# Moving the last group of adaLN weight loads and sums into the second block's input projection

## The chip, the cores and the metric

One Trainium2 chip, one core. The metric is the device time of one execution in microseconds: the median over the runs shown, beside one execution taken with the hardware profiler. Engines are named as in the profile: PE is TensorE, DVE is VectorE, ACT is ScalarE, POOL is GpSimd and SP is SyncE, which here issues all DMAs of the kernel. L1253 is line 1253 of the kernel before.

## The reference, cut to what matters

The kernel computes one hybrid decoder layer on x of 1024 tokens by 1024 channels in float32. The conditioning vector c gives six vectors of 1024 channels, and these shift, scale and gate the two halves of the layer:

```python
mod = silu(c) @ ada_w + ada_b
shift1, scale1, gate1, shift2, scale2, gate2 = split(mod, 6)
h = x * (1.0 + scale1) + shift1
z = h @ w_in                                 # 1024 x 3984
o = concat(hgrn2(z_h), gla(z_g), rwkv7(z_r)) @ w_out
x = layer_norm(ALPHA * x + (1.0 + gate1) * o)
h = x * (1.0 + scale2) + shift2
m = square(relu(h @ mlp_w_up)) @ mlp_w_down
x = layer_norm(ALPHA * x + (1.0 + gate2) * m)
```

The sixth vector, gate2, is needed only in the last line. The change moves the work that computes it.

## The kernel before, in words

The tokens go through in two blocks of 512, each of four tiles of 128. For each block there is an input projection (`z_block`, `z_rest`, `z_last`), the three mixers (`mix`, one tile after another with state carried along, in stages that overlap two tiles), the output projection with layer norm (`out_block`), and the MLP. Results of the input projection go to DRAM (`zr`, `zgc`, `zgt`, `zhc`, `zht`), and the mixers load them from there; they store theirs to `oD`, from which the output projection loads.

Every large product is made of three matmuls in a reduced float32 format. A weight slab of 128 rows is loaded (`slab`, tile `raw`, five buffers), ScalarE rounds it (`wh`, L1287), and VectorE takes the remainder (`wl`, L1288; four buffers of each). TensorE then does high by high, high by low and low by high (L1337 to L1339). The PSUM tile `dn` has four buffers. When a product is done, its tiles are copied, by ScalarE (L1382) and in the first block by VectorE in turn (L1384), to the tile `s2` (two buffers; the profile calls it `s`), and stored (L1386, L1388).

The six vectors of the conditioning are computed on VectorE. The weights come transposed, so that channel group q, 128 channels of the 6144, is one load of 128 by 1024 floats (512 KB) and one instruction that multiplies it by silu(c) and sums along the row:

```python
w = self.dt([P, D], "xt", 4)
ins = nc.sync.dma_start(w, self.A["ada_wt"][q * P:(q + 1) * P, :])
nc.vector.scalar_tensor_tensor(w, w, 1.0, self.cact, ALU.mult, ALU.mult, accum_out=self.sums[:, q:q + 1])
```

`xt` has four buffers, and silu(c) holds one of them until the last sum; three rotate among the loads. The first 16 channel groups (shift1 and scale1) are loaded in step with the first block's projection (`ada_first`). The other 32, eight for each of the four remaining vectors m = 2, 3, 4, 5, come from `ada_later(m)`, called in the program after the first block's mixers. For m = 2 and m = 5 (the gates) it also transposes the result in PSUM (tile `ml`, L1273) and stores it as a row to DRAM. Later `xt` tiles, in program order, are those of the output block (`ys`) and of the MLP.

The order in which instructions stand on each engine is not that of the program. At the end, `Order` lists all instructions with their dependences, walks through them with its own table of durations, and fixes one order for each engine, which the hardware then follows. An instruction's rank is its level (`level(n)`, lower first) and then its place in the program. ScalarE and VectorE take ready instructions that touch the dense products' pools (`feeds`, and `xt` is one of these pools' tiles) ahead of all others. Buffers of one tag are handed out in program order. Levels here: the first block's projection -1, its rest (`z_rest`) 0.5, the first block's mixers 0, the second block's projection 2 (`L_Z1`), `ada_later` 3 (`L_ADA`), the output block 0. So the second block's projection is the filler for the time of the first block's mixers, and the loads of `ada_later` go out whenever SP has nothing of a lower level to issue and an `xt` buffer is free.

ScalarE's two sets of activation tables are loaded in program order too (`act`): the exponentials of a stage stand behind the sigmoids of that stage, the last of which, of the tile G (L330), needs what the first block's projection stored last.

Of the kernel before, what the change touches and what calls it, by code (L numbers as in the profile page):

```python
# [25 lines left out]
KT = D // P  # L26
# [93 lines left out]
class Kern:  # L120
# [5 lines left out]
    def init(self, tc, ctx):  # L126
        self.tc, self.nc = tc, tc.nc
        self.psm = ctx.enter_context(tc.tile_pool(name="psm", bufs=2, space=PSUM))
        self.mp = ctx.enter_context(tc.tile_pool(name="mp", bufs=1))
        self.nid = 0  # L130
        self.table, self.head, self.group = None, None, []
        self.later, self.levels, self.first = [], [], None

# [1042 lines left out]
class Full(Kern):  # L1176
# [68 lines left out]
        self.sums = self.cp.tile([P, 48], F32, name="sums")  # L1245


    def ada_sum(self, q):
        nc = self.nc
        w = self.dt([P, D], "xt", 4)  # L1250
        ins = nc.sync.dma_start(w, self.A["ada_wt"][q * P:(q + 1) * P, :])
        self.first = ins if q == FIRST else self.first
        nc.vector.scalar_tensor_tensor(w, w, 1.0, self.cact, ALU.mult, ALU.mult, accum_out=self.sums[:, q:q + 1])  # L1253

# [8 lines left out]
            self.ada_sum(q)  # L1263
            self.ada_end(q, 1, plus)

    def ada_later(self, m):
        nc = self.nc
        for j in range(KT):
            self.ada_sum(8 * m + j)
        self.ada_end(8 * m, KT, 0.0 if m % 3 == 0 else 1.0)  # L1270
        if m % 3 == 2:
            ps = self.lps()
            nc.tensor.transpose(ps[0:8, 0:P], self.mod[:, 8 * m:8 * m + 8], self.ident)  # L1273
            row = self.dt([P, 512], "lnr", 2)[0:8, 0:P]
            nc.scalar.copy(row, ps[0:8, 0:P])
            nc.sync.dma_start(self.gD[m].rearrange("o (j p) -> (o j) p", p=P), row)
# [14 lines left out]
    def slab(self, ap, eng=None, tag="w"):  # L1291
        n = ap.shape[1]
        raw = self.dt([P, 512], "raw", RB)
        self.nc.sync.dma_start(raw[:, 0:n], ap)
        return self.split(raw[:, 0:n], tag, AB if tag == "a" else WB, n, eng=eng)


# [308 lines left out]
def build(tc, A):  # L1606
    with ExitStack() as ctx:
        k = Full(ctx, tc, A)
        k.level(-1)
        k.scratch()  # L1610
        k.ada_setup()
        k.z_block(0)
        k.level(0)
        k.setup_consts(A["consts"])
        k.level(L_Z0)
        k.z_rest(0)
        k.level(0)
        k.setup_mixers(A["masks"], A["wau"],
                       A["gla_alpha_up"][0], A["rwkv_g_up"][0], (A["rwkv_gn_g"], A["rwkv_gn_b"]))
        k.mix(0, M0)  # L1620
        k.level(L_ADA)
        for m in (2, 3, 4, 5):
            k.ada_later(m)
        k.level(L_Z1)
        k.z_block(1)
        k.z_rest(1)
        k.level(0)
        ys = k.out_block(0, False)
        k.z_last(1, (k.x_moving(1, j, True) for j in range(KT)))
        h = k.mlp_moving(ys, False)  # L1630
        k.mix(1, M1)
        k.tail(ctx)
        nch = FT // 4
        acc = [k.dt([P, D], "xt", 4) for _ in range(TPB)]
        for fc in range(nch):
            k.level(L_MLP + fc)
            k.mlp_chunk(fc, h, acc, False)
            if fc == OUT_AT:
                ys = k.out_block(1, True, L_MLP + fc + 2)
            k.level(L_MLP + fc + 1)  # L1640
            if fc == MOVE_AT:
                h1 = k.mlp_moving(ys, True)
        acc1 = [k.dt([P, D], "xt", 4, late=True) for _ in range(TPB)]
        k.level(L_MLP + nch)
        for fc in range(nch - 1):
            k.mlp_chunk(fc, h1, acc1, True)
            if fc == 0:
                k.level(L_MLP + nch + 1)
                k.mlp_end(0, acc)
                k.level(L_MLP + nch)  # L1650
        k.mlp_last(1, h1, acc1)
        Order(tc, k.later, k.levels).apply()
# [37 lines left out]
```

## Time and profile before

| | |
|---|---|
| median of 3 runs | 1487.52 us (1486.14 to 1488.55) |
| profiled execution | 1486.98 us |
| its span | 1485.2 us |
| mean granted TensorE clock | 0.981 |
| PE busy | 1406.1 us (95%) |
| DVE busy | 1055.1 us (71%) |
| ACT busy | 708.9 us (48%) |
| HBM read and written | 180.03 MB and 32.06 MB |

The times are of whole executions. The profiled one stands 1.8 us above its span, and 0.54 us below the median of the runs. The busy shares are averages over stages that differ: in the first 160 us the DMA engines are nearly full, from 220 to 480 us the mixers of the first block run beside the second block's projection, and beyond 600 us the MLP fills TensorE. What a moved piece of work costs or gives back has to be read from its own stage.

### The profile page before, as it was taken

What the parts mean: (1) busy time and instruction counts of PE and PEld (TensorE: products, weight loads), DVE (VectorE), ACT (ScalarE), POOL (GpSimd) and SP (SyncE); (2) the same over time, 40 slices, a digit from 0 to 9 for tenths busy, and PEclk for the clock granted to TensorE, in tenths of its full rate; (3) what the DMA queues carried; (4) which work ended last, traced back from release to release, by engine and by line L of the source; (5) the groups of instructions that cost most, each with busy time, mean ns of one, the idle gap of its engine ahead of it and who ended that gap; (6) DMA issues with size and microseconds to landing.
All of it is one profiled execution on the core that took longest, in us unless ns stands there. A gap on an engine that the chain in (4) does not pass through costs nothing.

```text
span 1485.2 us, 29273 instructions
## 1 busy us (share of the span) xinstructions
PE 1406.1 (95%) x11226; PEld 1124.2 (76%) x11226; DVE 1055.1 (71%) x2130; ACT 708.9 (48%) x1527; POOL 25.4 (2%) x32
## 2 busy tenths in 40 slices
PE   6998999999997798999999999999999999999996
PEld 5877877777876576777777778778887888888884
DVE  7787569697967577897979796474769434544478
ACT  3543355767674644747584844222433322333331
POOL 1000000000000000000000000000000000000004
PEclk9999999999998798999999999999999999999998
DMA  9998573544442557324242325563236333233331
GB/s 351 309 358 277 177 230 94 147 133 134 115 119 68 175 168 225 105 79 129 64 130 80 98 79 166 162 197 108 87 126 217 117 97 95 92 97 95 93 113 57
DMA packets 163292, 214.01 MB, mean 144 GB/s; under 512 B 39856, under 2 KB 90192, under 8 KB 163152
## 3 DMA queue, kind: packets, MB, share of 16 engines
q1 hardware_dynamic: 163152, 212.14, 45.7%
q8 instruction: 88, 1.44, 0.4%
q14 instruction: 52, 0.43, 0.1%
HBM read 180.03 MB, written 32.06 MB: 143 GB/s over the span
## 4 chain that ended last, share of the span: by engine, by line
PE 51%; DVE 4%; DMA 3%; ACT 2%; issue 1%; POOL 1%; SPq 0%; DVEq 0%; ACTq 0%; POOLq 0%
PE dn L1339 11%; PE dn L1338 11%; PE dn L1337 10%; PE tn L1338 5%; PE tn L1337 5%; PE tn L1339 5%; DMA lnr<-in_ln_b_dram 1%; PE ml L434 1%; DVE wl L1288 1%; DMA zht<-s 1%; DMA x1D<-xt 0%; DMA G<-zgt 0%; PE mr L598 0%; ACT wh L1287 0%; DVE xt L1471 0%
## 5 line engine op out<-in xcount | busy, mean ns | idle before, releaser
L1287 ACT CAST wh<-raw 128x512 fp32r<-128x512 f32 (+2 forms) x424 | 253.5, 599 | 500.4 <-PE dn L1339 215.9
L1288 DVE TENSOR_TENSOR wl<-raw,wh 128x512 fp32r<-128x512 f32 (+2 forms) x424 | 280.1, 664 | 293.2 <-ACT wh L1287 268.2
L1337 PE MATMUL dn<-wh,ah 128*128 128x512 f32 (+1 forms) x736 | 284.6, 390 | 8.5 <-ACT s L1382 3.9
L1338 PE MATMUL dn<-wl,ah 128*128 128x512 f32 (+1 forms) x736 | 287.2, 390 | 5.7 <-DVE wl L1288 5.7
L1339 PE MATMUL dn<-wh,al 128*128 128x512 f32 (+1 forms) x736 | 283.4, 390 | 3.8 <-DVE al L1513 3.8
L1337 PE MATMUL dn<-ah,wh 128*128 128x512 f32 x560 | 225.6, 404 | 16.1 <-ACT ah L1330 11.7
L1339 PE MATMUL dn<-ah,wl 128*128 128x512 f32 x560 | 225.9, 404 | 0.0
L1338 PE MATMUL dn<-al,wh 128*128 128x512 f32 x560 | 224.4, 401 | 0.0
L1337 PEld LDWEIGHTS dn<-wh,ah 128*128 128x128 f32 x736 | 139.0, 189 | 41.2 <-ACT s L1382 4.8
L1338 PEld LDWEIGHTS dn<-wl,ah 128*128 128x128 f32 x736 | 139.6, 190 | 32.6 <-DVE wl L1288 6.8
L1339 PEld LDWEIGHTS dn<-wh,al 128*128 128x128 f32 x736 | 139.0, 190 | 32.3 <-DVE al L1513 5.9
L1337 PEld LDWEIGHTS dn<-ah,wh 128*128 128x128 f32 x560 | 105.6, 189 | 41.9 <-ACT ah L1330 11.7
L1339 PEld LDWEIGHTS dn<-ah,wl 128*128 128x128 f32 x560 | 105.7, 189 | 22.4 <-issue 0.6
L1338 PEld LDWEIGHTS dn<-al,wh 128*128 128x128 f32 x560 | 105.8, 189 | 22.2 <-issue 0.5
L1337 PE MATMUL tn<-ah,wh 128*128 128x512 f32 x256 | 101.1, 395 | 0.0
L1338 PE MATMUL tn<-al,wh 128*128 128x512 f32 x256 | 101.1, 395 | 0.0
L1339 PE MATMUL tn<-ah,wl 128*128 128x512 f32 x256 | 100.7, 393 | 0.0
L1253 DVE SCALAR_TENSOR_TENSOR xt<-xt,xt 128x1024 f32<-128x1024 f32 x48 | 58.4, 1220 | 14.6 <-DMA xt<-in_ada_wt_dram 14.5
L157 ACT ACTIVATE ld<-ld 128x320 f32<-128x320 f32 (+1 forms) x120 | 54.5, 490 | 29.7 <-DVE ld L417 23.6
L1528 DVE TENSOR_TENSOR xt<-xt,dn 128x512 f32<-128x512 f32 x104 | 65.0, 680 | 0.1
L1339 PEld LDWEIGHTS tn<-ah,wl 128*128 128x128 f32 x256 | 48.2, 188 | 11.2
L1337 PEld LDWEIGHTS tn<-ah,wh 128*128 128x128 f32 x256 | 48.2, 188 | 11.1
(288 smaller groups left out, 1976.0 us busy)
## 6 DMA issues: line engine op xcount, KB each, us to landing
raw<-in_mlp_w_up_dram SPq DMA_DIRECT2D x128, 256.0 KB
raw<-in_mlp_w_down_dram SPq DMA_DIRECT2D x128, 256.0 KB
xt<-in_ada_wt_dram SPq DMA_DIRECT2D x48, 512.0 KB
raw<-in_w_in_dram SPq DMA_DIRECT2D x64, 256.0 KB
raw<-in_w_in_dram SPq DMA_DIRECT2D x48, 192.0 KB
raw<-in_w_out_dram SPq DMA_DIRECT2D x32, 256.0 KB
raw<-in_w_in_dram SPq DMA_DIRECT2D x32, 196.0 KB
raw<-in_xt_dram SPq DMA_DIRECT2D x24, 256.0 KB
```

Of the source, the lines that this page charges most:

```text
L157: ins = nc.scalar.activation(out, in_, func, **kw)
L434: nc.tensor.matmul(ps[r, p * 32:p * 32 + 32], e[:, p * 128 + 32 * g:p * 128 + 32 * g + 32], R[:, :, p, 16 * g:16 * g + 16], start=True, st ...
L1253: nc.vector.scalar_tensor_tensor(w, w, 1.0, self.cact, ALU.mult, ALU.mult, accum_out=self.sums[:, q:q + 1])
L1287: nc.scalar.copy(hi[:, 0:n], src)
L1288: (eng or nc.vector).tensor_tensor(lo[:, 0:n], src, hi[:, 0:n].bitcast(F32), ALU.subtract)
L1337: nc.tensor.matmul(ps, lh, rh, start=first, stop=False)
L1338: nc.tensor.matmul(ps, lh, rl, start=False, stop=False)
L1339: nc.tensor.matmul(ps, ll, rh, start=False, stop=last)
L1528: nc.vector.tensor_tensor(acc[t][:, cs], acc[t][:, cs], ps, ALU.add)
```

## The change

`ada_later(5)`, the eight loads and sums of gate2, is called after the second block's projection instead of with the other three, so that its level is 2 and its rank is behind that projection. Each of its eight loads is also ordered behind one of the last 24 weight slabs of the projection (the two products for `zgt` and that for `zhc`): load j behind slab 3j of these, counted from 0. `slab` keeps the list of slab loads for it. Both kinds of load are issued by SP, so this is an order on SP's queue and no wait on data. What is computed is the same.

```diff
-        self.nid = 0
+        self.nid, self.slabs = 0, []
...
-    def ada_sum(self, q):
+    def ada_sum(self, q, slab=None):
         nc = self.nc
         w = self.dt([P, D], "xt", 4)
         ins = nc.sync.dma_start(w, self.A["ada_wt"][q * P:(q + 1) * P, :])
+        if slab is not None:
+            self.after(ins, [slab])
...
-    def ada_later(self, m):
+    def ada_later(self, m, slabs=()):
         nc = self.nc
         for j in range(KT):
-            self.ada_sum(8 * m + j)
+            self.ada_sum(8 * m + j, slabs[j * len(slabs) // KT] if slabs else None)
...
-        self.nc.sync.dma_start(raw[:, 0:n], ap)
+        self.slabs.append(self.nc.sync.dma_start(raw[:, 0:n], ap))
...
         k.level(L_ADA)
-        for m in (2, 3, 4, 5):
+        for m in (2, 3, 4):
             k.ada_later(m)
         k.level(L_Z1)
         k.z_block(1)
         k.z_rest(1)
+
+        k.ada_later(5, k.slabs[-24:])
         k.level(0)
         ys = k.out_block(0, False)
```

## Rows read from the trace of the kernel before

**Rows 1.** The page, busy time of each engine, share of the span, instructions.

```profile
PE 1406.1 (95%) x11226; PEld 1124.2 (76%) x11226; DVE 1055.1 (71%) x2130; ACT 708.9 (48%) x1527; POOL 25.4 (2%) x32
```

**Rows 2.** Stretches: from:to, length, busy by engine (instructions), granted clock, DMA share, GB/s.

```profile
148.00:217.00 69.00, 67.11 (x308) 56.34 (x307) 41.06 (x94) 27.82 (x54) 0.00 (x0) 0.98 0.65 199
217.00:320.00 103.00, 100.67 (x1137) 76.22 (x1139) 87.15 (x208) 70.45 (x167) 0.00 (x0) 1.00 0.45 133
320.00:355.00 35.00, 34.89 (x699) 26.53 (x691) 30.88 (x89) 21.68 (x56) 0.00 (x0) 1.00 0.33 91
355.00:375.00 20.00, 19.50 (x129) 16.91 (x128) 12.25 (x27) 18.11 (x51) 0.00 (x0) 1.00 0.67 207
375.00:420.00 45.00, 44.07 (x818) 37.70 (x817) 42.65 (x112) 25.85 (x69) 0.00 (x0) 1.00 0.37 105
420.00:440.00 20.00, 18.78 (x249) 14.95 (x248) 9.39 (x20) 17.76 (x44) 0.00 (x0) 1.00 0.52 147
440.00:490.00 50.00, 37.40 (x570) 28.70 (x568) 32.95 (x63) 25.78 (x68) 0.00 (x0) 0.78 0.19 64
```

**Rows 3.** PE's waits, 430 to 500 us: us in total, times, longest.

```profile
PE dn L1302 <- DMA raw<-oD: 4.9, 3, 2.7
```

**Rows 4.** ACT's timeline: start, us, instruction, [idle before it, what ended that].

```profile
144.16 0.48 ACT L1382 COPY s<-dn 128x392 f32<-128x392 f32 x1 [6.70 <-DMA zgt<-s]
...
217.25 0.74 ACT L157 ACTIVATE ld<-G 128x640 f32<-128x640 f32 x1 [0.82 <-DMA G<-zgt]
```

**Rows 5.** DVE's timeline, three of the eight sums of the last group.

```profile
128.99 1.23 DVE L1253 SCALAR_TENSOR_TENSOR xt<-xt,xt 128x1024 f32<-128x1024 f32 x1 [0.73 <-DMA xt<-in_ada_wt_dram]
...
139.94 1.23 DVE L1253 SCALAR_TENSOR_TENSOR xt<-xt,xt 128x1024 f32<-128x1024 f32 x1 [5.58 <-DMA xt<-in_ada_wt_dram]
...
155.79 1.21 DVE L1253 SCALAR_TENSOR_TENSOR xt<-xt,xt 128x1024 f32<-128x1024 f32 x1
```

**Rows 6.** SP's timeline: start, us, DMA issue, how many.

```profile
123.33 0.38 SPq L1251 DMA_DIRECT2D xt<-in_ada_wt_dram  x1
...
139.99 0.34 SPq L1386 DMA_DIRECT2D zgt<-s  x1
...
149.35 0.33 SPq L1251 DMA_DIRECT2D xt<-in_ada_wt_dram  x1
...
488.82 2.57 SPq L1314 DMA_DIRECT2D raw<-oD  x5
```

**Rows 7.** PE's timeline, four starts after a pause.

```profile
130.75 0.55 PE L665 MATMUL mr<-consts,BK 128*128 128x128 f32 x3 [0.82 <-DVE bon L635]
...
141.72 0.44 PE L1338 MATMUL dn<-wl,ah 128*128 128x392 f32 x1 [1.75 <-DVE wl L1288]
144.70 0.70 PE L1337 MATMUL dn<-wh,ah 128*128 128x392 f32 x1 [2.54 <-ACT s L1382]
...
166.59 0.50 PE L1337 MATMUL dn<-ah,wh 128*128 128x512 f32 x1 [1.58 <-ACT s L1382]
```

**Rows 8.** Stretches of 4 us around these pauses, columns as in rows 2.

```profile
140.00:144.00 4.00, 0.44 (x1) 0.19 (x1) 4.00 (x9) 0.00 (x0) 0.00 (x0) 0.99 0.67 207
144.00:148.00 4.00, 3.30 (x16) 2.85 (x18) 0.96 (x6) 1.21 (x3) 0.00 (x0) 0.50 0.95 295
148.00:152.00 4.00, 4.00 (x20) 3.78 (x19) 3.01 (x7) 2.19 (x8) 0.00 (x0) 0.65 1.00 350
```

**Rows 9.** Slab loads (L1294) in three stretches: issue ns min/median/max, first to last start.

```profile
L1294 SPq DMA_DIRECT2D raw<-in_w_in_dram x6: 327/331/438, 328.5 to 344.1; - x6
...
L1294 SPq DMA_DIRECT2D raw<-in_w_in_dram x6: 332/370/468, 352.3 to 371.2; - x6
...
L1294 SPq DMA_DIRECT2D raw<-in_w_in_dram x13: 327/328/490, 373.1 to 424.5; - x13
```

**Rows 10.** DVE's timeline behind 420 us.

```profile
425.05 0.83 DVE L463 TENSOR_TENSOR ld<-ld,K 128x640 f32<-128x640 f32 x1 [4.68 <-ACT ld L157]
```

**Rows 11.** The page, the group of all 48 sums: busy, mean ns | idle before, releaser.

```profile
L1253 DVE SCALAR_TENSOR_TENSOR xt<-xt,xt 128x1024 f32<-128x1024 f32 x48 | 58.4, 1220 | 14.6 <-DMA xt<-in_ada_wt_dram 14.5
```

## The prediction

> **What bounds the kernel now.** I read the page's busy table first, then the stretches of the front 490 us, then the timelines where TensorE stops. Over the span PE is busy for 95% [rows 1], so time can only come from its pauses, or from a chain that holds it up. The stretches say where that is. From 217 to 440 us PE is idle for 2.33 + 0.11 + 0.50 + 0.93 + 1.22 = 5.1 us of 223 [rows 2]: the first block's mixers (level 0) and the second block's input projection (level 2, the filler) share it without a gap. From 440 to 490 us it is idle for 12.6 us and its granted clock averages 0.78 [rows 2]: the filler has run out, and the output projection waits for what the mixers store (its transposes waited 4.9 us for it) [rows 3]. So the whole front ends when the first block's mixers end. Their last part starts when the first block's projection is through: ScalarE's sigmoid of G at 217.25 waits for the load of G [rows 4], which waits for that projection's stores, and from 148 to 217 us PE is busy for 67.1 of 69 us [rows 2]. A pause of PE ahead of 217 us is therefore paid in full, and so is whatever delays the mixers behind it.
>
> **The change, part by part.** The sums of group 5 are the last 8 of 48. In the trace they start on DVE from 128.99 to 155.79 us [rows 5], and their loads are issued from 123.33 to 149.35 us [rows 6].
>
> *What leaves the front.* Eight loads of 512 KB, eight sums of 1.22 us and eight accumulator reads of some 0.08 us (1.3 us a pair), and what stands behind them. Three pauses hang on them:
> - The third sum waits 5.58 us for its weights, until 139.94 [rows 5]. DVE runs in order, so the split of the next slab of the projection stands behind it, and PE waits 1.75 us for that split [rows 7].
> - PE then waits 2.54 us for ScalarE's eviction [rows 7], which itself had waited 6.70 us for the store of zgt to land [rows 4]. That store was issued only at 139.99 [rows 6], among these loads, with the DMA engines at 0.67 to 1.00 [rows 8]. The same eviction at the next product's end, with no such load about, costs PE 1.58 us [rows 7], and I leave that much here too: 2.54 - 1.58 = 0.96 us come back.
> - Behind these pauses the granted clock falls: 0.50 from 144 to 148 and 0.65 from 148 to 152 us [rows 8]. At 0.50 that is the lower level, 1.2 GHz. The loss against full clock is 0.50 x 4 + 0.35 x 4 = 3.4 us.
>
> A smaller one: PE waits 0.82 us at 130.75 for a DVE instruction [rows 7] that stands behind the first of these sums, which was late by 0.73 us itself [rows 5]. Sum: 1.75 + 0.96 + 3.4 + 0.8 = 6.9 us. Below, it is 1.75 + 0.82 = 2.6 us, if the eviction's wait stays whole and drops the clock as before; above, 1.75 + 2.54 + 3.4 + 0.82 + 1.58 = 10.1 us, if the next eviction is quick too. I take 6.9: the two pauses ahead of the clock's fall are 4.3 us together, while the one of 1.58 us at 166 us was followed by no fall (the 0.98 of 148 to 217 us [rows 2] is the 1.4 us just counted).
>
> The first 40 loads stay where they are: the group's own loads could not start before 123 us, so nothing ahead of that moves.
>
> *What comes to the back.* Load j of the eight may be issued behind slab 3j of the last 24 (counted from 0). In the trace these slabs are issued 6, 6 and 13 to a stretch, of which the first is one too early [rows 9], so that two sums come to the stretch of 320 to 355 us, two to 355 to 375, and four to 375 to 420 (an estimate, a few microseconds for landing added). Each takes 1.3 us of DVE, 10.4 in all. DVE is busy there for 30.88 of 35, 12.25 of 20 and 42.65 of 45 us [rows 2]. With 2.6, 2.6 and 5.2 us more, the first two still fit (33.5 and 14.9), and the third runs over by 42.65 + 5.2 - 45 = 2.9 us. Bounds: 0, as the stretch behind it has DVE busy for 9.4 of 20 us [rows 2] and a wait of 4.68 us on ScalarE at its head [rows 10] that could take the overflow, and as PE hardly waits here at all; 10.4 us, if each sum stands ahead of a mixer's step on the chain, which the kernel's planner favours, since it takes what feeds the dense products first. I take 2.9, from the rows of just this stretch.
>
> *The queues.* SP issues each load in 0.33 us [rows 6], 2.6 us in all, behind slabs whose own rate is one in some 4 us (24 in 96) [rows 9]: SP has room, and the slabs have five buffers. A load moves 0.52 MB, at the 350 GB/s of 148 to 152 us [rows 8] 1.5 us of the DMA engines, which are busy for 0.33 to 0.67 there [rows 2]; what is queued behind it, a slab or the mixers' small transfers, comes up to 1.5 us later. Slabs are prefetched; for the mixers' I take 0, and at most 1.5 us for each of the two or three loads that could meet them. A load waits for no buffer: three rotate, and the sum three loads back is done by then. Cover gone, it would hold SP's whole queue.
>
> *Whoever needs the group.* gate2 is used at the end of the MLP, and its transpose stands behind the last mixer's PSUM tiles in tile order, before and after. Nothing: the sums end at some 412 us, ahead of that. The buffers then pass to the output block, whose first loads of the mixers' results are issued at 488.82 [rows 6]; if the sums came as late as that, it would wait for them.
>
> *A rule against it.* DVE was held for 5.58 us by one load, and by all 48 sums together for 14.6 us [rows 11], 0.30 us a sum. The Trainium skill (TensorE: Matmul & The Clock Gate, on engine queue depths) says that ACT and DVE are strict FIFO; by that rule, and the trace agrees with its 5.58 us, every sum that comes ahead of its load holds the mixers too. At 0.30 us for each of eight, the back would cost 2.4 us more and the change would bring 1.6 us. I leave it out of the sum, because the loads of before run at DMA shares of 0.67 to 1.00 [rows 8] and the moved ones would at 0.33 to 0.67 [rows 2]; it goes to the slower rival.
>
> **Sum.** -6.9 + 2.9 = -4.0 us. Against the profiled execution's 1486.98 us that is 1483.0; this execution stands 0.54 us below the median of 1487.52, so against the median, by which I give the time, 1483.5 us.
>
> **The rivals.**
> 1. *The back is free and the front gives all.* The overflow goes into the 4.68 us wait, and the clock stays up: -7 to -10 us, 1477.5 to 1480.5. For it: PE pauses for 5.1 us in 223, so few delays of DVE reach it. Against: with DVE at 95% from 375 to 420 us, four sums have no gap to go to.
> 2. *Slower: the sums stand in the mixers' chain.* Place: DVE from 320 to 420 us. All 10.4 us are paid, and 2.4 us for loads that are late: 12.8 - 6.9 = +5.9, 1493.4 us. It decides once a sum costs the mixers more than 6.9/8 = 0.86 us, two thirds of its length. For it: DVE is the fullest engine beside PE there, and runs the sums first; and the mixers' chain (invert, two chunks, next tile) passes DVE every few microseconds. Against: the attention's share of DVE's work has 4.68 us of slack at 425 us, and a step on the chain meets on average half a sum.
> 3. *Nothing to measure: the front's gain is not there.* The eviction waits for SP's order rather than for the loads (between 134 and 140 us SP issues the mixers' gathers as well), and the clock drops again. -2.6 + 2.9 = +0.3, 1487.8 us.
>
> **How the numbers follow.** A measurement of this kernel tells some 0.2%, 3 us, from no change. Chances: the forecast 0.55 (within -7.5 and +0.5: 0.36 of it faster, 0.17 same, 0.02 slower), rival 1 0.13 (faster), rival 2 0.20 (0.18 slower, 0.02 same), rival 3 0.12 (0.01, 0.08, 0.03). Sums: faster 0.50, same 0.27, slower 0.23. The range reaches to rival 1's end and nearly to rival 2's: 1477.5 to 1492.5. Some 0.13 is left out, most of it rival 2 with longer waits. The forecast's own range is 1480 to 1488.
>
> **What would show it.** In the new profile, no wait of DVE for these weights between 128 and 160 us; PE without the two pauses at 140 to 145 us and the granted clock at 1.00 from 144 to 152; the sigmoid of G some 7 us ahead of 217.25; eight sums on DVE between some 315 and 410 us, each starting without a wait. The mixers' last store and the first transposes of the output block would come 4 us earlier. The prediction is wrong if that sigmoid does not move, or if it moves and the output block comes no earlier: then the gain was given back between 310 and 480 us, and DVE's waits and the steps behind the sums would say where.

## The result and the profile after

The changed kernel takes 1496.04 us (median of 7 runs, 1493.96 to 1503.02) against 1487.03 us for the kernel before in runs beside it (7 runs, 1483.94 to 1488.55). The ratio is 1.0068, with a 95% interval of 1.005 to 1.0086: slower by 9.0 us, where 4 us less had been forecast. The profiled execution took 1493.96 us, its span 1492.0 us, so that it shows +7.0 us of the 9.0; it is the fastest of the seven. A time read from a timeline is that of one execution. Two executions of the changed kernel's order stand 3.2 us apart at the output block (last experiment), so a difference of that size between two timelines is not taken for an effect here.

**The front gained more than forecast.** The stretches around the old pauses and the first projection's end, in the changed kernel (columns as in [rows 2]):

```profile
140.00:144.00 4.00, 4.00 (x25) 4.00 (x24) 3.45 (x14) 2.87 (x9) 0.00 (x0) 1.00 0.46 146
144.00:148.00 4.00, 4.00 (x24) 4.00 (x23) 2.74 (x12) 1.02 (x2) 0.00 (x0) 1.00 0.60 165
148.00:152.00 4.00, 4.00 (x24) 4.00 (x24) 1.63 (x4) 1.51 (x4) 0.00 (x0) 1.00 0.44 122
148.00:217.00 69.00, 68.55 (x308) 56.30 (x308) 37.76 (x71) 31.79 (x59) 0.00 (x0) 1.00 0.63 193
```

PE has no pause left from 140 to 152 us, and its granted clock stays at 1.00, where it was 0.50 and 0.65 [rows 8]. ScalarE's timeline shows the mixers starting earlier, at 207.16 instead of 217.25 us [rows 4], by 10.1 us (9.8 in two further executions of this order):

```profile
207.16 0.74 ACT L157 ACTIVATE ld<-G 128x640 f32<-128x640 f32 x1 [0.68 <-DMA G<-zgt]
```

**The first block's mixers gave it all back.** SP's timeline, two of the eight moved loads, the output block's first loads and the first residual loads at the end of the first block's MLP:

```profile
318.68 0.49 SPq L1251 DMA_DIRECT2D xt<-in_ada_wt_dram  x1
...
342.44 0.43 SPq L1251 DMA_DIRECT2D xt<-in_ada_wt_dram  x1
...
490.14 2.57 SPq L1316 DMA_DIRECT2D raw<-oD  x5
...
963.85 0.93 SPq L1537 DMA_DIRECT2D raw<-x1D  x2
```

The output block starts at 490.14 us, 1.3 us later than before [rows 6]: of 10.1 us gained, the stretch from 207 to 490 us has lost 11.4 (14.4 in a second execution of the same order). The attention's four stores to DRAM, one for each tile, show it on its way: 10.8 us earlier than before at the first, 5.4 at the second, 2.2 later at the third, 1.4 later at the fourth. The stretch is that of the moved sums, and DVE's timeline shows how they start (idle time before them in brackets):

```profile
323.98 1.23 DVE L1255 SCALAR_TENSOR_TENSOR xt<-xt,xt 128x1024 f32<-128x1024 f32 x1 [2.19 <-DMA xt<-in_ada_wt_dram]
...
332.41 1.23 DVE L1255 SCALAR_TENSOR_TENSOR xt<-xt,xt 128x1024 f32<-128x1024 f32 x1 [1.15 <-DMA xt<-in_ada_wt_dram]
...
346.29 1.23 DVE L1255 SCALAR_TENSOR_TENSOR xt<-xt,xt 128x1024 f32<-128x1024 f32 x1 [0.42 <-DMA xt<-in_ada_wt_dram]
```

The first waits 2.19 us for weights issued 5.3 us before it, the third 0.42 us for weights issued 3.9 us before. DVE's waits from 300 to 420 us, in total, times and longest, are

```profile
DVE xt L1255 <- DMA xt<-in_ada_wt_dram: 5.5, 5, 2.2
```

So the wait that had been cured in the front, DVE held by weights that have not landed, stands in the mixers now. The stretches there, for [rows 2]:

```profile
320.00:355.00 35.00, 32.03 (x402) 25.11 (x401) 26.89 (x75) 20.92 (x55) 0.00 (x0) 1.00 0.51 148
355.00:375.00 20.00, 18.47 (x125) 16.44 (x123) 16.44 (x38) 15.75 (x44) 0.00 (x0) 1.00 0.71 222
375.00:420.00 45.00, 42.41 (x722) 34.13 (x723) 39.07 (x103) 24.49 (x65) 0.00 (x0) 1.00 0.53 155
420.00:440.00 20.00, 19.61 (x305) 15.75 (x305) 11.55 (x23) 13.73 (x35) 0.00 (x0) 1.00 0.22 55
440.00:490.00 50.00, 36.01 (x576) 28.05 (x572) 34.14 (x65) 28.07 (x72) 0.00 (x0) 0.66 0.22 73
```

From 320 to 440 us PE is idle for 7.5 us, where it was for 2.8; from 440 to 490 us for 14.0 instead of 12.6, at 0.66 of its clock instead of 0.78. Against full clock that is 4.7 + 1.4 + 0.12 x 50 = 12.1 us, about what the stretch lost.

**And the part behind lost seven more.** The first residual load stood at 955.59 us before (the same view of the kernel before):

```profile
955.59 0.85 SPq L1535 DMA_DIRECT2D raw<-x1D  x2
```

It is 8.3 us later now, and only 1.3 of that came from ahead of the output block: from there to this load it takes 473.7 us instead of 466.8. No instruction of the change stands in that part. Its order, though, is not the one of before: the planner fixes one order for the whole kernel, and a moved group changes what it chooses later. PE's timeline shows one place, in the kernel before and in the changed one:

```profile
690.11 0.50 PE L1337 MATMUL dn<-wh,ah 128*128 128x512 f32 x1 [1.47 <-ACT ah L1511]
```

```profile
694.52 0.50 PE L1339 MATMUL dn<-wh,ah 128*128 128x512 f32 x1 [2.74 <-ACT ah L1513]
```

and the stretches of the changed kernel there and at a second place like it show the clock, which before was 1.00 in both:

```profile
680.00:720.00 40.00, 36.61 (x425) 27.08 (x424) 36.18 (x77) 27.88 (x70) 0.00 (x0) 0.96 0.34 97
840.00:880.00 40.00, 38.60 (x568) 29.96 (x569) 33.80 (x70) 26.76 (x65) 0.00 (x0) 0.96 0.24 72
```

That is 0.04 x 40 = 1.6 us in each of the two, 3.2 of the 7.0. Where the rest goes was not followed.

### The profile page after: what moved, and what is told of

Same layout as the page of the kernel before. It is cut to its first block, busy times and chain, and to the rows that moved or that the text cites. A ratio compares the mean times of both kernels' runs of the same rounds, so it can differ in the third digit from the quotient of the medians.

```text
span 1492.0 us, 29255 instructions
## 1 busy us (share of the span) xinstructions
PE 1413.1 (95%) x11226; PEld 1129.0 (76%) x11226; DVE 1055.3 (71%) x2130; ACT 712.1 (48%) x1527; POOL 25.5 (2%) x32
## 4 chain that ended last, share of the span: by engine, by line
PE 50%; DVE 6%; ACT 3%; DMA 2%; issue 1%; POOL 1%; DVEq 0%; SPq 0%; ACTq 0%; POOLq 0%
PE dn L1341 10%; PE dn L1340 10%; PE dn L1339 10%; PE tn L1341 5%; PE tn L1340 5%; PE tn L1339 5%; DVE wl L1290 1%; DMA lnr<-in_ln_b_dram 1%; PE ml L434 1%; ACT L154 0%; DVE xt L1473 0%; ACT wh L1289 0%; DVE xt L1530 0%; PE tn L1304 0%; DVE xt L1603 0%
## 5 line engine op out<-in xcount | busy, mean ns | idle before, releaser
L1339 PE MATMUL dn<-ah,wh 128*128 128x512 f32 x560 | 226.6, 405 | 13.3 <-ACT ah L1332 11.7
L1339 PEld LDWEIGHTS dn<-ah,wh 128*128 128x128 f32 x560 | 106.5, 190 | 38.7 <-ACT ah L1332 11.7
L1255 DVE SCALAR_TENSOR_TENSOR xt<-xt,xt 128x1024 f32<-128x1024 f32 x48 | 58.5, 1221 | 15.1 <-DMA xt<-in_ada_wt_dram 14.9
L1340 PEld LDWEIGHTS tn<-al,wh 128*128 128x128 f32 x256 | 48.1, 188 | 11.2
```

Of the source, the lines that this page charges most:

```text
L1339: nc.tensor.matmul(ps, lh, rh, start=first, stop=False)
L1340: nc.tensor.matmul(ps, lh, rl, start=False, stop=False)
```

## The experiments

Two things are mixed in the changed kernel: where eight loads and eight sums stand, and the planner's new order of everything else. The first four runs keep the order of the kernel before. The planner plans that kernel, and then, in three of them and in the run called the sums in DVE's gaps, the eight loads are moved on SP's list and the eight sums on DVE's, with the one small instruction that adds up the group's result; every other instruction stands on its engine as before. Two runs take the new order in one part of the kernel alone. The first four share 24 runs of the kernel before (median 1484.42 us, 1481.52 to 1489.48), the last four share 23 (1486.09 us, 1479.51 to 1488.28). Differences are taken between medians; the ratios compare all runs, and the two can differ a little. In the diffs, `...` stands for what is left out.

The theory was that all of the sums' DVE time and all of their waits are paid, because DVE's order holds the mixers; its rivals were that the waits alone cost, that the sums alone do, and that neither does and the new order is to blame.

### The front's gain by itself

The group's loads and sums stay at their old places, with loads and sums of 8 of the 1024 columns. This leaves out most of gate2's sum.

```diff
-        ins = nc.sync.dma_start(w, self.A["ada_wt"][q * P:(q + 1) * P, :])
-        nc.vector.scalar_tensor_tensor(w, w, 1.0, self.cact, ...)
...
+        n, m = (8, 8) if q >= 40 else (D, D)
+        ins = nc.sync.dma_start(w[:, 0:n], self.A["ada_wt"][q * P:(q + 1) * P, 0:n])
...
+        self.adds.append(nc.vector.scalar_tensor_tensor(w[:, 0:m], w[:, 0:m], 1.0, self.cact[:, 0:m], ...
```

> The order of the kernel before on every engine, instruction for instruction; only the eight loads and sums of the last group, in their old place, are cut to 8 of 1024 columns (so gate2 is not the reference's). Nothing is added behind 160 us. My theory: the front's gain of some 10 us passes through the mixers and the MLP whole: 1477 us, with the sigmoid of G some 10 us ahead of 217 and the transposes of the output block at 479 us in place of 489. Rival: the mixers or the MLP have another bound, and most of the gain is lost on the way: 1484 to 1487 us.

Measured: 1477.93 us (1475.14 to 1482.49), ratio 0.9956 (0.9935 to 0.9977), -6.5 us: the theory came, its rival did not. The sigmoid of G, on ScalarE's timeline, and the output block's first loads, on SP's:

```profile
209.21 0.74 ACT L157 ACTIVATE ld<-G 128x640 f32<-128x640 f32 x1 [0.56 <-DMA G<-zgt]
```

```profile
480.15 2.57 SPq L1325 DMA_DIRECT2D raw<-oD  x5
```

The first is 8.0 us ahead of the kernel before [rows 4], where some 10 had been expected, the second 8.7 us [rows 6]. What the front gains does reach the output block when nothing is brought to the back.

### The group moved by hand

Each load stands behind slab 3j, each sum where the planner's own arithmetic has it landed (`LAG` 0).

```diff
...
+        for j in range(8):
+            s = slabs[3 * j]
+            sp.insert(sp.index(s) + 1, loads[j])
+            t = self.span[s][0] + 2 * DMA_ISSUE + DMA_START + 1456 + DMA_END + LAG
+            dve.insert(next(n for n, k in enumerate(dve) if k not in adds and self.span[k][0] >= t), adds[j])
```

> The order of the kernel before on every engine, with only the eight loads taken to behind every third of the last 24 slabs on SP, and the eight sums to the places on VectorE where the planner's own arithmetic has each load landed. My theory (part of the loss is the moved work, part is that the planner wrote a new order for everything behind it): the output block starts within 2 us of 490, as in the changed kernel, but the MLP loses nothing more: 1487 to 1490 us. Rival (all of the loss comes with the moved work itself): 1495 us, as the changed kernel. Second rival (the new order alone eats the gain): 1480 us or less.

Measured: 1499.3 us (1496.09 to 1501.97), ratio 1.0094 (1.0076 to 1.0112), +14.9 us. DVE's waits from 300 to 440 us, the first of the sums, and the output block's start:

```profile
DVE xt L1270 <- DMA xt<-in_ada_wt_dram: 11.8, 8, 3.0
```

```profile
325.87 1.23 DVE L1270 SCALAR_TENSOR_TENSOR xt<-xt,xt 128x1024 f32<-128x1024 f32 x1 [2.87 <-DMA xt<-in_ada_wt_dram]
```

```profile
320.40 0.48 SPq L1267 DMA_DIRECT2D xt<-in_ada_wt_dram  x1
...
501.66 1.47 SPq L1332 DMA_DIRECT2D raw<-oD  x3
```

Every one of the eight sums waits for its weights. The output block starts 12.8 us later than before: worse than the changed kernel, with not an instruction reordered but the group's own. So the placement is enough to lose, and the new order is not what loses here. The theory (1487 to 1490 us) and both rivals missed; the nearest was the one that all of the loss comes with the moved work.

### The same with the sums 5 us later

`LAG` is 5000 ns; the loads stay.

> As the kernel moved by hand, but each sum stands 5 us later on VectorE, so that its load has landed. My theory: the waits of VectorE for these loads go (5.5 us in the changed kernel), the sums' 10.4 us of VectorE stay: 3 to 6 us faster than the kernel moved by hand, some 1483 us. Rival (what counts is VectorE's time, the waits lie beside other waits): as the kernel moved by hand within 2 us.

Measured: 1487.72 us (1483.13 to 1491.01), ratio 1.0016 (1.0004 to 1.0029), +3.3 us. No wait for these weights is left on DVE, and the output block starts at

```profile
490.37 2.57 SPq L1332 DMA_DIRECT2D raw<-oD  x5
```

11.3 us earlier than with the early sums, whose waits were 11.8 us together. The waits were paid about one for one; the theory had expected 3 to 6 us. The rest goes with the sums: 490.37 against 480.15 of the front alone, 10.2 us. The prediction put eight sums at 10.4 us, 1.3 us each. Where sums stand back to back on DVE's timeline, though, they start 1.15 us apart (the run with the sums in the gaps shows three such starts), so that eight take 9.2 us.

### The same waits with small sums

Loads and places as in the group moved by hand, the loads whole, the sums over 8 columns (which leaves out most of gate2's sum again).

```diff
-        nc.vector.scalar_tensor_tensor(w, w, 1.0, self.cact, ...)
...
+        n, m = (1024, 8) if q >= 40 else (D, D)
...
+        self.adds.append(nc.vector.scalar_tensor_tensor(w[:, 0:m], w[:, 0:m], 1.0, self.cact[:, 0:m], ...
```

> As the kernel moved by hand, with the loads whole but each sum over 8 of 1024 columns (so gate2 is not the reference's): the waits for the loads stay, 9 us of VectorE's time go. My theory (both cost about their length times 0.7): 6 us faster than the kernel moved by hand, some 1482 us. Rival (only the waits count): as the kernel moved by hand within 2 us. Rival (only the sums' time counts): some 1478 us, as the front alone.

Measured: 1489.61 us (1485.61 to 1492.95), ratio 1.0032 (1.0019 to 1.0046), +5.2 us. DVE's waits from 300 to 440 us and the output block's start:

```profile
DVE xt L1275 <- DMA xt<-in_ada_wt_dram: 10.5, 7, 4.7
```

```profile
493.63 2.57 SPq L1338 DMA_DIRECT2D raw<-oD  x5
```

Waits with hardly a sum behind them cost 493.63 - 480.15 = 13.5 us, for 10.5 us of waiting. The pair of runs without waits (front alone, later sums) gives 10.2 us for the sums; this one and the group moved by hand give 501.66 - 493.63 = 8.0. Those are single executions. The medians of the four runs agree better: the sums cost 1487.72 - 1477.93 = 9.8 us without waits and 1499.3 - 1489.61 = 9.7 with them, the waits 1499.3 - 1487.72 = 11.6 us with full sums and 1489.61 - 1477.93 = 11.7 with small ones. So both are paid in full, beyond what the theory (0.7 of their length) and either rival had. What the loads' own traffic costs is not isolated by these four, as no run has the whole loads with neither waits nor sums.

Where this goes on PE is seen in the stretch from 300 to 440 us: front alone, later sums, moved by hand.

```profile
300.00:440.00 140.00, 136.21 (x2087) 110.40 (x2086) 112.97 (x282) 97.58 (x251) 0.00 (x0) 1.00 0.40 117
```

```profile
300.00:440.00 140.00, 131.29 (x1993) 106.76 (x1992) 114.30 (x283) 90.39 (x236) 0.00 (x0) 0.98 0.47 142
```

```profile
300.00:440.00 140.00, 122.55 (x1792) 99.31 (x1790) 107.57 (x265) 81.45 (x209) 0.00 (x0) 0.95 0.44 131
```

PE is idle for 3.8, 8.7 and 17.5 us, and its clock comes down to 0.98 and 0.95, another 2.8 and 7.0 us. From the first run to the third that is 13.7 + 7.0 = 20.7 us, of the 21.5 by which the output block moves (480.15 to 501.66). PE, 97% busy without the sums, does not work on through DVE's delays. PE's timeline in the third run has the longest of its waits, 4.08 us, and DVE's the step that it waits for; the same step in the front alone stands below them:

```profile
328.40 0.76 PE L434 MATMUL ml<-Rs,ld 128*32 128x32 f32 x40 [4.08 <-DVE Rs L423]
...
327.53 0.81 DVE L423 TENSOR_TENSOR Rs<-ld,Qz 128x640 f32<-128x640 f32 x1
```

```profile
323.64 0.81 DVE L423 TENSOR_TENSOR Rs<-ld,Qz 128x640 f32<-128x640 f32 x1
```

This is a matmul of the mixers, waiting for DVE's step of the mixers. That step stands behind the first of the moved sums, which waited 2.87 us itself (325.87 above), and comes 3.9 us later than in the front alone. PE's next two waits, of 3.8 and 2.6 us, are for DVE's steps of the mixers too. As each engine's order is fixed, the filler behind such a matmul on PE's list waits with it.

### The new order, one part at a time

Both plans are made, the one of before and the one of the changed kernel, and joined on each engine at the planned start of the output block's first load. The first run takes the new plan ahead of that and the old one behind; the second takes the old one ahead, with the sums at their old place, and the new one behind. In the cut, `t` is the planned start at which they are joined.

```diff
...
+            front = {k for k in self.order[e] if self.span[k][0] < t}
+            self.order[e] = [k for k in other.order[e] if k in front] + [k for k in self.order[e] if k not in front]
```

> Two plans joined: each engine follows the changed kernel's order for all that the old plan starts before the output block's first load, and the order of the kernel before for the rest. What is computed is the same. My theory (up to 490 us the changed kernel is 1 to 2 us late; the 6 to 7 us more that it loses between 600 and 960 us come from the new order of the MLP and the second block's mixers, which the planner wrote because its clock was shifted, and not from the moved work): 1 to 3 us slower than before, with the output block's start and the second block's residual loads shifted by the same 1 to 2 us. Rival (the later loss follows from the moved work, whatever the order behind it): 7 to 10 us slower, as the changed kernel.

Measured: 1491.82 us (1488.24 to 1493.8), ratio 1.0042 (1.0028 to 1.0056), +5.7 us. Output block and residual load:

```profile
493.08 2.57 SPq L1331 DMA_DIRECT2D raw<-oD  x5
...
961.46 0.93 SPq L1554 DMA_DIRECT2D raw<-x1D  x2
```

The output block is 4.3 us later than before, more than expected, and more than in the changed kernel's profile (1.3), although the order up to there is the same. The two profiles differ in the granted clock from 300 to 440 us, changed kernel first:

```profile
300.00:440.00 140.00, 132.46 (x1986) 106.24 (x1986) 112.07 (x278) 88.16 (x228) 0.00 (x0) 1.00 0.48 139
```

```profile
300.00:440.00 140.00, 132.37 (x1958) 106.54 (x1957) 111.07 (x275) 87.03 (x223) 0.00 (x0) 0.98 0.47 138
```

That is 0.02 x 140 = 2.8 us, about the 2.9 us between them. It stands in one place: behind pauses of PE near 376 us the clock is 0.79, 0.50 and 0.86 in the three stretches of 4 us from 376 to 388 us here, and 1.00 in the changed kernel's profile. From the output block to the residual load it takes 468.4 us, near the 466.8 of before.

> The other way round: the old order, with the sums at their old place in the front, up to the output block's start, and the changed kernel's order behind it. My theory: 5 to 8 us slower than before, all of it between 600 and 960 us. Rival: as before within 2 us.

Measured: 1491.87 us (1488.85 to 1494.39), ratio 1.0044 (1.0026 to 1.0061), +5.8 us, with the group at its old place:

```profile
488.33 2.57 SPq L1331 DMA_DIRECT2D raw<-oD  x5
...
963.03 0.93 SPq L1554 DMA_DIRECT2D raw<-x1D  x2
```

The output block starts 0.5 us earlier than before, the residual load comes 7.4 us later. The new order behind the output block costs this by itself, as the theory had it. It comes every time: from the output block's first loads to this one it takes 465.6 to 468.9 us in the seven profiles with the old order there, and 473.7 to 474.7 in the three with the new one. PE's timeline has the pause of the changed kernel again, and the clock falls behind it, in 688 to 704 and in 848 to 864 us:

```profile
693.68 0.80 PE L1354 MATMUL dn<-wh,ah 128*128 128x512 f32 x1 [2.74 <-ACT ah L1530]
```

```profile
688.00:696.00 8.00, 5.26 (x18) 3.76 (x18) 7.97 (x20) 6.34 (x14) 0.00 (x0) 0.84 0.44 140
696.00:704.00 8.00, 8.00 (x55) 6.23 (x53) 7.54 (x15) 3.82 (x8) 0.00 (x0) 0.94 0.27 80
848.00:856.00 8.00, 6.69 (x79) 5.17 (x80) 5.47 (x11) 6.03 (x16) 0.00 (x0) 0.87 0.42 131
856.00:864.00 8.00, 8.00 (x55) 5.85 (x55) 5.92 (x15) 2.23 (x5) 0.00 (x0) 0.70 0.11 32
```

Against full clock that is 8 x (0.16 + 0.06 + 0.13 + 0.30) = 5.2 us of the 7.9 lost in this part (474.7 against 466.8); in the kernel before, all four stood at 1.00. In the changed kernel's second execution the pause of 2.74 us is there again, with 0.91 from 680 to 720 us, but from 840 to 880 us the clock stays at 1.00; only the first place shows each time. Which of the planner's choices lengthens the pause was not tried. The two parts make 5.7 + 5.8 = 11.5 us, where the changed kernel loses 9.0, and 10.5 in the second measurement below; as each part is known to some 2 us either way, that is no contradiction.

### The sums in DVE's gaps

The plan of before, the first five loads behind slabs 0, 3, 6, 9 and 12, three behind the attention's store of the third tile; the sums stand ahead of instructions of the mixers for which DVE waited in the trace of before (two in the second tile, three ahead of the third tile's L463, which had waited 4.68 us [rows 10], three in the fourth tile). The first list names places for the loads, the second for the sums.

```diff
...
+        for x, n in reversed(list(zip([slabs[0], slabs[3], slabs[6], slabs[9], slabs[12]] + 3 * [k.od[2]], loads))):
+            sp.insert(sp.index(at[x.ins.name]) + 1, n)
+        for x, n in zip([k.o1[2], k.st[2]] + 3 * [k.kh[2]] + 3 * [k.o1[6]], adds):
+            dve.insert(dve.index(at[x.ins.name]), n)
```

> The order of the kernel before on every engine, with the eight loads behind slabs of the last 24 (five) and behind the third tile's store (three), and the eight sums put just ahead of instructions for which VectorE waits on ScalarE in the trace of before: one each near 359 and 364 us, three at 425 us (a wait of 4.68 us) and three at 481 us (6.57 us). My theory (VectorE is on the path from 300 to 440 us, so that its time is paid wherever it is not waiting anyway): the front's gain is kept, 5 to 7 us faster than before, within 2 us of the front alone. Rival (any work on VectorE there is paid): within 2 us of the kernel moved by hand with later sums, 2 to 4 us slower than before.

Measured: 1479.19 us (1476.06 to 1483.72), ratio 0.9965 (0.9951 to 0.9979), -6.9 us. This is faster than both kernels and what the theory had; by the ratio it is 5.2 us, with an interval of 3.1 to 7.3. DVE's timeline at the third tile, and SP's:

```profile
414.52 1.22 DVE L1271 SCALAR_TENSOR_TENSOR xt<-xt,xt 128x1024 f32<-128x1024 f32 x1
...
415.67 1.22 DVE L1271 SCALAR_TENSOR_TENSOR xt<-xt,xt 128x1024 f32<-128x1024 f32 x1
...
416.81 1.22 DVE L1271 SCALAR_TENSOR_TENSOR xt<-xt,xt 128x1024 f32<-128x1024 f32 x1
...
419.30 0.83 DVE L464 TENSOR_TENSOR ld<-ld,K 128x640 f32<-128x640 f32 x1 [1.26 <-ACT ld L158]
```

```profile
483.13 2.57 SPq L1333 DMA_DIRECT2D raw<-oD  x5
...
948.71 0.93 SPq L1554 DMA_DIRECT2D raw<-x1D  x2
```

Three sums stand where DVE was idle for 4.68 us, and 1.26 us of idle time are left: three sums took 3.42 us of it. No sum waits for its weights. The output block starts 5.7 us earlier than before, and the residual load comes 6.9 us earlier. The output block is still 3.0 us later than in the front alone, a difference of the size by which executions differ; the totals, -6.9 and -6.5 us, show no cost of the moved group. Three of the loads are issued later here than in the run with the later sums, so the sums' places are not the only difference between those two.

### The planner told of the landing

The changed kernel, with 2 us added in the planner's arithmetic of the eight loads, meant as a later landing.

```diff
-                        free = end + DMA_END
+                        free = end + DMA_END + (2000 if self.ins[k].name in self.slow else 0)
```

> The changed kernel, with 2 us added in the planner to the landing of the eight moved loads; it writes a new order throughout. My theory: the waits of VectorE for these loads (5.5 us in the changed kernel) all but go, and the output block starts some 4 us earlier, at 484 to 487 us; what the new order does behind 600 us is open, -3 to +7 us. In all 1480 to 1490 us. Rival (the planner's places for the sums do not matter): 1494 us, as the changed kernel.

Measured: 1496.56 us (1493.14 to 1498.91), ratio 1.0076 (1.0055 to 1.0096), +10.5 us. DVE's waits from 250 to 500 us, the output block and the residual load:

```profile
DVE xt L1258 <- DMA xt<-in_ada_wt_dram: 6.3, 6, 2.2
```

```profile
493.35 2.57 SPq L1319 DMA_DIRECT2D raw<-oD  x5
...
967.12 0.93 SPq L1540 DMA_DIRECT2D raw<-x1D  x2
```

The rival seems to have come, but the run does not test it. The edit changes `free`, the time at which the planner hands a load's buffers on. The time from which it lets a sum start is taken from `end` a few lines on, which the edit leaves alone:

```python
at = end + SEEN[e][ENGINES.index(self.eng[m])]
```

The order that comes out is that of the changed kernel on every engine. So whether a better number for the landing would mend the placement stays open. What the run gives is a second measurement of the changed kernel: +10.5 us beside +9.0. Its sigmoid of G stands at 207.41 us, its output block at 493.35 instead of 490.14, and the part behind takes 473.8 us, as in the first.

## Why the prediction was wrong

- **What bounds the kernel** was right: a pause of PE ahead of 217 us is paid in full, and so is a delay of the mixers. The front alone shows the first (the sigmoid 8.0 us earlier, the output block 8.7), the group moved by hand the second.
- **The front's gain, 6.9 us within 2.6 to 10.1,** was right in kind and somewhat small in size. At the sigmoid of G it is 8.0 to 9.4 us in the runs that keep the old order and 9.8 to 10.1 in the new order; the front alone gains 6.5 us in the whole time. The pauses went and the clock stayed up, as the steps had it. The term that was mis-sized is the eviction's wait: PE's waits of 2.54 and 1.58 us both went, as in the upper bound, where 1.58 us had been left in each place.
- **The back's cost, 2.9 us,** is the step that failed. It was argued from DVE's busy time in three stretches: what does not fill a stretch costs nothing, and PE hardly waits there. The sums' own time cost 9.8 us in the medians (10.2 in the profiles) of the later sums, near the upper bound of 10.4. That bound itself was a little high, as sums on end start 1.15 us apart and not 1.3. DVE's idle time in those stretches was no free room: a sum put ahead of a step of the mixers shifts what follows, whatever room comes later. That PE was idle for only 5.1 us of 223 [rows 2] was read as evidence that few of DVE's delays reach it. It was only evidence that the order of before had few: with the sums put in, PE stops for the mixers' steps that come late, as its wait of 4.08 us in the group moved by hand shows. The forecast named the 4.68 us of [rows 10] as a place for the overflow. It is one for sums put right ahead of it, as the sums in the gaps show. With the later sums DVE's longest wait for that step is still 4.7 us: the sums ahead of it took nothing out of it.
- **The loads' lateness was left out of the sum,** 2.4 us by 0.30 us a sum from all 48 [rows 11]. That average is taken over sums of which most had been loaded long before. In the changed kernel it was 5.5 us for eight, by hand 11.8, or 0.7 to 1.5 us a sum, and by hand it was paid in full. The reason given for leaving it out, that the DMA engines would be less busy, went by the average of a stretch. The share while one load is under way is another. The first moved load of the changed kernel, from issue to the start of its sum, and the first of the group in the kernel before [rows 5, 6] (columns as in [rows 2], the share of the DMA engines is the last but one):

```profile
318.68:323.98 5.30, 5.30 (x32) 3.96 (x32) 2.84 (x12) 2.92 (x7) 0.00 (x0) 1.00 0.96 260
```

```profile
123.33:128.99 5.66, 5.58 (x55) 4.79 (x54) 4.93 (x12) 1.25 (x4) 0.00 (x0) 1.00 0.93 281
```

The moved load met engines as full as the old one did. The rule weighed in the prediction was the one to follow: the Trainium skill (TensorE: Matmul & The Clock Gate, engine queue depths) has DVE as a strict FIFO, and the runs agree, with 11.3 us paid for 11.8 us of waits.
- **SP's queue and the DMA engines, nothing:** not contradicted, and not isolated. The sums in the gaps keep all eight whole loads and lose nothing against the front alone in the totals; the later sums lose 9.8 us, where eight sums on end take 9.2.
- **All behind 490 us a mere shift** was assumed and not argued, and it failed: the new order of the tail costs some 7 us by itself (7.4 us later at the residual load with the old order ahead of it).
- **The rivals.** The slower one, that the sums stand in the mixers' chain, is what came, at a chance of 0.20 and 1493.4 us. Its point of decision, 0.86 us a sum, was passed: the changed kernel pays 11.4 us up to the output block, 1.4 us a sum. The prediction's sign of being wrong, that the sigmoid of G moves while the output block comes no earlier, is what the profile shows. That rival's time is 2.6 us from the measured one partly by luck: its front is too small, its waits are too small, and it has nothing for the order of the tail.

The account of the changed kernel, in the profiles: -10.1 us in the front, +11.4 us by the output block, +7.0 us by the end of the first block's MLP, -1.5 us behind it, together +6.8 us, the difference of the spans. In the second execution they are -9.8, +14.4, +7.0 and -2.0 us, together +9.5 us (spans 1494.7 against 1485.2). By the price of the hand-made runs, eight sums of 1.15 us and waits of 5.5 to 6.3 us would make 14.7 to 15.5 us for the second term; the front-only run, of the same order up to there, paid 14.1. So sums and waits account for it within what executions differ, and the lower 11.4 us go for the most part with the higher clock of that one profile from 376 to 388 us.

## What to carry to other kernels

Before work goes to an engine with idle time, look at what ends each idle stretch: time between two steps of one chain is no room unless the work is put right where the engine waits, and its operands have landed by then. A TensorE that hardly waits says that the present order fits, not that a delay elsewhere would be covered: each engine keeps its order, and a filler behind a late step is late too. And when a planner makes the order, compare the part that the change does not touch as well, or move the instructions by hand in the old order to see what the move alone is worth. Where a planner's number is changed, look first whether the order changed with it: otherwise the time says nothing of that number.

## What the hardware showed beside this

How long a load of 512 KB issued by SP takes went only loosely with how full the DMA engines were. In the changed kernel and the group moved by hand, DVE waited for 13 of them, until 3.6 to 5.9 us after their issue. Of the five with a DMA share above 0.9 in that time, four took 5.3 to 5.9 us and one 4.4; of the four at 0.50 to 0.62, three took 3.6 to 4.3 us and one 5.3. The Trainium skill (DMA: Bandwidth & Descriptors, on the anatomy of one DMA) has a fit of fixed and variable cost for DMAs that GpSimd issues. By that fit 2.0 + 524288/436000 = 3.2 us would be an estimate for 512 KB. The loads here are issued by SP, beside other traffic, and all 13 took longer.

One longer pause of PE, 2.74 us instead of 1.47, came with a granted clock of 0.84 and 0.94 in the two stretches of 8 us that hold and follow it, where the shorter one stood in stretches at 1.00 (the run with the new order behind the output block, and the kernel before). This pause cost more than its own length; that of 1.58 us at 166 us [rows 7] was followed by no fall. Nor does the same order always fare the same: from 376 to 388 us the clock fell to 0.50 in two of the three executions of the changed kernel's front, and stayed at 1.00 in the third, with pauses of PE there in all three.
